# A two-layer block on one core: low-rank paths of the time mix from unmixed features, keys before the other products

## The chip, the cores and the metric

The kernel runs on one core of a Trainium2 chip. TensorE multiplies, VectorE (DVE), ScalarE (ACT) and GpSimd (POOL) do the elementwise work, and transfers from HBM are issued mostly on the queue of SyncE (SP). The metric is the device time of one execution in microseconds; before the change the median of three runs was 1236.0 us (1233.78 to 1236.62).

## The reference

256 tokens of 1024 features pass through two blocks in float32: the first has latent attention with retention, cross-attention to 256 memory rows and a mixture of 32 experts; the second has an attention and pooling mixer, a gated feed-forward layer, an RWKV-7 time mix, and a second feed-forward layer. The change lies in the time mix and at the join of the two blocks. Cut to what matters there:

```python
xx = _token_shift(h) - h
xr, xw, xk, xv, xa, xg = [h + xx * mu[i] for i in range(6)]
r, k, v = xr @ w_r, xk @ w_k, xv @ w_v                 # 1024 x 1024 each
w = -softplus(-(w0 + tanh(xw @ w1) @ w2)) - 0.5        # decays, rank 64
a = sigmoid(a0 + (xa @ a1) @ a2)                       # rates, rank 64
g = sigmoid(xg @ g1) @ g2                              # gate, rank 160
kk = k * k_k / max(norm(k * k_k), 1e-12)               # by heads of 64
k = k * (1 + (a - 1) * k_a)
decay = exp(-exp(w))
# per token and head: state = state * decay + (state @ -kk) (kk * a)^T + v k^T;  y = state @ r
y = group_norm(y) * ln_w + ln_b + sum(r * k * r_k) * v
return (y * g) @ w_o
```

## The kernel before

Features stand with the 1024 features over partitions in eight blocks of 128 and the 256 tokens along the free axis ("feature-major"). A fast product is made of three single-pass products (`mm3`): each operand is split into a rounded part, which ScalarE casts to fp32r (line 363), and a rest, which VectorE subtracts (line 364); where `self.sub` is set, POOL does. `mm` on operands left in float32 is one product, which leaves two records in the trace. Weights come through a ring of five raw buffers (`w`, `NRAW`) by `wchunk`, are split into `ws` buffers, and a product lands in one of four PSUM banks `acc` or four `ps`.

The time mix (from 773 us) norms x, transposes it to hF and takes dF, the difference with the token before. The mixes h + xx * mu for the rates, the gate and v are made on POOL (`mix_apart`, lines 1504 and 1505), those for r, the decays and k on VectorE. The order written is: r, low ranks of decays and rates, gate, decays `sg`, rates `av`, their running sums and exponentials (`em`, `ep`, `be`), then k chunk by chunk with the removal of its part along kk (`k_evac`), with v's chunks in between. Tokens are cut into chunks of 64, those into blocks of 32. L, the products of keys with keys inside the blocks, is turned by a stream transpose (`Ll`), and the unit triangular matrix I + L is inverted for all 128 blocks at once by a substitution of 31 steps with two VectorE operations each (`Xl`). The inverse is transposed back (`Lc`, then `X`), joined to the 64-wide inverse, and the chunk loop carries the state over four chunks. `ar` holds the decayed removal directions and r; `kb` the keys and the rates' keys; "products" (`p`) are kb with ar; "turned" (`t`) are transposes `BK`; "corners" (`c`) and the gate (`g`) are further generators.

Tile places instructions on each engine in the order that a simulated timeline gives; `behind` (`issue_after`) holds a piece back until a named instruction has been placed. Which step of which generator comes between the keys' chunks, the removals, the substitution's steps and the chunks is the table `BETWEEN`: a letter is one step. In the first block, the experts' last group (g == 7) is followed by a branch for tokens over an expert's 32 places (`overflow`, not taken with these inputs); SyncE takes part in it, and the next layer's weights `hy_w_in` were issued behind it.

Of the kernel before, what the change touches and what calls it, by code (L numbers as in the profile page):

```python
# [19 lines left out]
P = 128  # L20
# [189 lines left out]
class Block:  # L210
    def __init__(self, ctx, tc, I, C, out, dbg=None, phases="ABCDEFG"):
# [12 lines left out]
        self.held = {}  # L224
# [20 lines left out]
        if "C" in phases:  # L245
# [3 lines left out]
            with tc.tile_pool(name="pC", bufs=1, reuse_waits="tile") as self.pp:  # L249
                x = self.phase_c(x, o)  # L250
# [748 lines left out]
    def phase_c(self, x, o):  # L999
# [86 lines left out]
        for g in range(8):  # L1086
# [86 lines left out]
    def overflow(self, x, r, gain, over, acc):  # L1173
# [3 lines left out]

        raw = lambda n: self.wp.tile([P, CW], F32, tag="w", bufs=NRAW, name=self.nm("ow"))[:, :n]
# [281 lines left out]
    def phase_f(self, x, with_ffn):  # L1460
# [37 lines left out]
        def mix_apart(i):  # L1498

            f = Feat(self, 8, "k4", 8, side)  # L1500
            for b in range(0, 8, 2):
                xm = k4("xm", "uv", 2)[:, :512].rearrange("p (k c) -> p k c", k=2)
                m = mu[:, i * 8 + b : i * 8 + b + 2].unsqueeze(2).broadcast_to([P, 2, T])
# [3 lines left out]
            return f  # L1507

# [10 lines left out]
        def rows(ap, n, extra=None):  # L1519

            r = self.wp.tile([P, CW], F32, tag="w", bufs=NRAW, name=self.nm("w"))
            nc.sync.dma_start(r[:n], ap)
            m = n
            if extra is not None:
                nc.sync.dma_start(r[n : n + 1], extra.unsqueeze(0))
                m = n + 1
            return self.wsplit(r[:m].rearrange("p (k c) -> p k c", k=2))

        def small_split(n):
            return [self.pp.tile([P, T], F32R, tag=f"lo{s}", bufs=2, name=self.nm("lo"))[:n] for s in range(2)]  # L1530

        def low_rank(f, w1):
# [641 lines left out]
```

## Time and profile before

| | us |
|---|---|
| median of 3 runs | 1236.0 (1233.78 to 1236.62) |
| the profiled execution | 1233.26 |
| its span in the trace | 1231.5 |
| TensorE busy | 1127.2 (92%), 7070 records |
| VectorE, ScalarE, POOL busy | 703.1, 574.8, 219.8 |
| time mix, from the norm's first transpose to the chunk loop's first product | 773.9 to 964.9 |
| experts' output done, next layer's first product | 471.1, 475.3 |

The span is what the trace covers of the profiled execution; the 1.8 us around it belong to its time. TensorE records can overlap, so sums of their lengths are more than the time they take; an interval between starts is exact. The granted clock of a stretch is given as a share of full speed.

### The profile page before, as it was taken

Reading aid. Unit: us, or ns where it says so; the run is one execution under the profiler, and the core shown is the slowest. Engines: PE = TensorE matmul, PEld = TensorE weight load, DVE = VectorE, ACT = ScalarE, POOL = GpSimd, SP = SyncE. Lnnn points to the kernel's source line nnn. Section 1 sums busy time; section 2 is a strip of 40 time slices with the busy share of each in tenths; the row PEclk is TensorE's granted clock in tenths of the full one; section 3 lists DMA queues with packets and bytes.
Section 4 is the critical chain, followed back from the end, with each engine's and each line's share of the span. In section 5 each row is a group of like instructions: output and inputs, shape, how many; then the busy total and the mean of one; then the engine's idle time right before and its main releaser. Section 6 shows DMA issues by size and latency. Waiting matters only on the chain. (4 is left out here: it accounts for less than half of the span.)

```text
span 1231.5 us, 18724 instructions
## 1 busy us (share of the span) xinstructions
PE 1127.2 (92%) x7070; PEld 874.4 (71%) x7070; DVE 703.1 (57%) x1332; ACT 574.8 (47%) x1116; POOL 219.8 (18%) x192
## 2 busy tenths in 40 slices
PE   6999999979988878999999999678998989999998
PEld 5778878744333225888888888677976977888887
DVE  4978565541211105875766666895766556766665
ACT  5667555411000004684645454447675355555452
POOL 3101000000000010300100000587476820000000
PEclk9999999989999988999999999798996999999999
DMA  8533596889999995543556655033312114756661
GB/s 282 169 118 118 173 386 212 299 312 409 409 409 409 409 394 174 172 136 121 188 188 188 188 188 171 26 106 102 121 50 84 46 36 154 224 187 188 189 190 67
DMA packets 125153, 246.04 MB, mean 200 GB/s; under 512 B 11665, under 2 KB 66353, under 8 KB 125058
## 3 DMA queue, kind: packets, MB, share of 16 engines
q1 hardware_dynamic: 123250, 240.52, 56.6%
q0 software_dynamic: 1520, 4.01, 1.0%
q8 instruction: 57, 0.93, 0.3%
q10 hardware_dynamic: 288, 0.26, 0.1%
q14 instruction: 38, 0.31, 0.1%
HBM read 243.70 MB, written 1.05 MB: 199 GB/s over the span
## 5 line engine op out<-in xcount | busy, mean ns | idle before, releaser
L364 DVE TENSOR_TENSOR ws<-w,ws 128x1024 fp32r<-128x1024 f32 (+5 forms) x341 | 329.0, 979 | 161.1 <-ACT ws L363 160.2
L363 ACT CAST ws<-w 128x1024 fp32r<-128x1024 f32 (+6 forms) x365 | 288.2, 804 | 222.1 <-issue 83.8
L312 PE MATMUL ps<-fp,ws 128*128 128x512 f32 (+1 forms) x1472 | 255.1, 334 | 0.2
L312 PEld LDWEIGHTS ps<-fp,ws 128*128 128x128 f32 x1472 | 221.9, 190 | 31.3 <-DVE fp L187 0.6
L312 PE MATMUL acc<-ws,f 128*128 128x512 f32 (+1 forms) x696 | 177.5, 408 | 13.6 <-ACT ws L363 7.4
L312 PEld LDWEIGHTS acc<-ws,f 128*128 128x128 f32 x696 | 132.3, 195 | 44.2 <-ACT ws L363 9.0
L326 ACT ACTIVATE s<-ps 128x256 f32<-128x256 f32 (+2 forms) x114 | 47.0, 414 | 217.7 <-PE ps L312 217.7
L312 PE MATMUL acc<-ws,h 128*128 128x512 f32 x528 | 124.1, 391 | 0.0
L312 PEld LDWEIGHTS acc<-ws,h 128*128 128x128 f32 x528 | 97.7, 188 | 21.0
L312 PE MATMUL acc<-f,ws 128*128 128x256 f32 x480 | 70.9, 304 | 16.5 <-DVE ws L364 10.2
L312 PE MATMUL ps<-we,xs 128*32 128x512 f32 x512 | 77.1, 606 | 3.4 <-DMA we<-in_experts_dram 2.0
L312 PEld LDWEIGHTS acc<-f,ws 128*128 128x128 f32 x480 | 65.6, 207 | 19.7 <-DVE ws L364 12.1
L347 POOL TENSOR_TENSOR rs_r<-rs_v,mhalf 128x2 f32<-128x2 f32 (+3 forms) x26 | 24.4, 944 | 301.8 <-DVE kan L338 181.8
L1112 DVE TENSOR_TENSOR xs<-ps,cols 128x256 f32<-128x256 f32 x32 | 13.6, 425 | 101.6 <-PE ps L312 101.5
L312 PE MATMUL acc<-ws,o 128*128 128x512 f32 x192 | 48.1, 406 | 1.3 <-ACT ws L363 1.2
L312 PEld LDWEIGHTS ps<-Pm,x 128*128 128x128 f32 x256 | 32.2, 200 | 23.0 <-issue 18.8
L312 PE MATMUL acc<-ws,mf 128*128 128x512 f32 x192 | 47.9, 399 | 0.0
L329 DVE TENSOR_TENSOR s<-ps,s 128x256 f32<-128x256 f32 x80 | 33.5, 421 | 24.5 <-ACT s L326 24.5
L312 PE MATMUL ps<-we,hT 128*32 128x512 f32 x256 | 36.9, 622 | 10.5 <-DMA rowD<-in_rowD_dram 6.7
L312 PEld LDWEIGHTS ps<-we,xs 128*32 128x32 f32 x512 | 15.6, 110 | 42.0 <-issue 25.9
L312 PEld LDWEIGHTS acc<-ws,o 128*128 128x128 f32 x192 | 36.3, 193 | 10.1 <-ACT ws L363 1.6
L347 POOL TENSOR_TENSOR rx<-rs_v,mhalf 128x2 f32<-128x2 f32 x6 | 7.3, 1208 | 191.9 <-DVE rs_v L338 106.3
(406 smaller groups left out, 1481.6 us busy)
## 6 DMA issues: line engine op xcount, KB each, us to landing
we<-in_experts_dram SPq DMA_DIRECT2D x192, 512.0 KB, 10.2
w<-in_ffn_w_gate_dram SPq DMA_DIRECT2D x44, 512.0 KB, 4.3
w<-in_ffn_w_up_dram SPq DMA_DIRECT2D x44, 512.0 KB, 3.7
w<-in_ffn_w_down_dram SPq DMA_DIRECT2D x44, 512.0 KB, 3.6
w<-in_hy_w_in_dram SPq DMA_DIRECT2D x20, 512.0 KB, 3.8
w<-in_w_in_dram SPq DMA_DIRECT2D x16, 512.0 KB, 4.6
w<-in_cross_w_kv_dram SPq DMA_DIRECT2D x16, 512.0 KB, 3.6
w<-in_rw_w_o_dram SPq DMA_DIRECT2D x10, 512.0 KB, 3.6
```

Source lines behind the costliest of these rows:

```text
L312: return self.nc.tensor.matmul(out, lhsT, rhs, start=start, stop=stop, skip_group_check=True)
L326: self.nc.scalar.activation(out, in_, func, **kw)
L329: self.nc.vector.tensor_tensor(out, a, b, op)
L347: self.rooted = self.nc.gpsimd.tensor_tensor(r, v, self.mhalf[:, :n], ALU.pow).ins
L363: i = self.nc.scalar.copy(a, src)
L364: j = (sub or self.nc.vector).tensor_tensor(b, src, a.bitcast(F32), ALU.subtract)
L1112: return nc.vector.tensor_tensor(xs[:, 2 * b : 2 * b + 2, :], ps.rearrange("p (k c) -> p k c", k=2), gb, ALU.mult)
```

## The change

The decays, rates and the gate are no longer taken from mixed and split features. Since (h + xx * mu) @ w = h @ w + xx @ (mu * w), their low-rank products are raw float32 products of hF with the weights and of dF with weights scaled by mu on VectorE (`scaled`); decays and rates share one 128-column pass. w2, a2, g2 and v are raw float32 products too, so their weights and features are not split. k and r stay split. Keys come first; r, v, the gate's second product, the products with kb and the turned matrices are steps between the substitution's. POOL no longer mixes or splits there. In the first block, the first four chunks of `hy_w_in` are issued ahead of the branch, whose code uses one weight buffer in place of several.

```diff
 BETWEEN = dict(
-    keys=("v", "", "", "v", "", "", "", "v"),
-    removals=("v", "v", "", ""),
-    substitution="vcvvpgpggtgtppgttppt",
-    chunks=(("", "", "tt"), ("p", "p", ""), ("", "", ""), ("", "", "")),
+    keys=("", "", "", "", "", "", "", ""),
+    removals=("r", "", "", ""),
+    substitution={0: "r", 4: "r", 8: "rc", 12: "r", 16: "r", 20: "r", 24: "r", 28: "pvpvpvtptvpvvvpvttggggtt"},
+    chunks=(("", "", ""), ("p", "p", ""), ("", "", ""), ("", "", "")),
 )
...
     def wchunk(self, w, k0, nk, c0, ncol):
 
+        if (k0, nk, c0, ncol) in self.early:
+            return self.early.pop((k0, nk, c0, ncol))
...
             if g == 7:
 
+                if with_next:
+
+                    new = {(k0, 2, 0, 512): self.wchunk(I["hy_w_in_2"][0], k0, 2, 0, 512) for k0 in (0, 2, 4, 6)}
+                    self.early.update(new)
+                ow = self.wp.tile([P, CW], F32, tag="w", bufs=NRAW, name=self.nm("ow"))
                 most = nc.values_load(mxi[0:1, 0:1], min_val=0, max_val=T)
                 with self.tc.If(most > 32):
-                    self.overflow(x, r, gain, over, acc)
+                    self.overflow(x, r, gain, over, acc, ow)
...
-        def mix_apart(i):
...
-                nc.gpsimd.tensor_tensor(xm, dF[:, b : b + 2, :], m, ALU.mult)
-                nc.gpsimd.tensor_tensor(xm, xm, hF[:, b : b + 2, :], ALU.add)
-                self.split_to(*f.blk(b, 2), xm, nc.gpsimd)
...
+        def scaled(r, parts):
+
+            nk = r.shape[1]
+            m = self.s2(nk * r.shape[2]).rearrange("p (k c) -> p k c", k=nk)
+            return m, [
+                nc.vector.tensor_tensor(
+                    m[:, :, c0 : c0 + n], r[:, :, c0 : c0 + n], mu[:, i * 8 + k0 : i * 8 + k0 + nk].unsqueeze(2).broadcast_to([P, nk, n]), ALU.mult
+                )
+                for i, k0, c0, n in parts
+            ]
...
+        ws = [scaled(wl[:, k0 : k0 + 4], ((1, k0, 0, 64), (4, k0, 64, 64)))[0] for k0 in (0, 4)]
+        pw = self.psb(T)
+        for k in range(8):
+            self.mm(pw, wl[:, k, :], hF[:, k, :], k == 0, False)
+        for k in range(8):
+            self.mm(pw, ws[k // 4][:, k % 4, :], dF[:, k, :], False, k == 7)
...
+        self.act(uw[:64], pw[:64], AF.Tanh)
+        nc.vector.tensor_copy(ua[64:], pw[64:])
+        fk = mix(2)
...
-                self.mm3(po, [q[:, t * P : (t + 1) * P] for q in uw], ws[c], True, True)
+                self.mm(po, uw[:, t * P : (t + 1) * P], w2[:65, c * 512 : c * 512 + 512], True, True)
...
+        def r_evac(j, ps):
+            sl = slice(2 * j, 2 * j + 2)
+            bo = self.s2(512)
+            self.tt(arx(1, sl), p3(ps), fl(ep[:, sl, :, 1:65]), ALU.mult)
             nc.gpsimd.tensor_tensor(p4(bo), f4(ar[:, sl, :, 1, :]), keys(sl), ALU.mult)
...
+        fv = [self.pp.tile([P, D], F32R, tag=f"f{s}", bufs=self.nf, name=self.nm("fv")).bitcast(F32).rearrange("p (k c) -> p k c", k=4) for s in (0, 1)]
+        for k in range(8):
+            self.stt(fv[k // 4][:, k % 4, :], dF[:, k, :], mu[:, 24 + k : 25 + k], hF[:, k, :], ALU.mult, ALU.add)
...
+                        for f_, w_ in ((hF, r[:, k1 + k]), (dF, m[:, k])):
+                            self.mm(pg[:, t], f_[:, kk, t * P : (t + 1) * P], w_, kk == 0 and t == 0 and f_ is hF, kk == 7 and f_ is dF)
...
+        def values():
+            for c in range(2):
+                ps = [self.psa(512) for _ in range(2)]
+                for k0 in range(0, 8, 2):
+                    w = self.wchunk(I["w_v"], k0, 2, c * 512, 512)
+                    for k in (k0, k0 + 1):
+                        for t in range(2):
+                            self.mm(ps[t], fv[k // 4][:, k % 4, t * P : (t + 1) * P], w[:, k - k0], k == 0, k == 7)
...
-        steps = {"v": chain.from_iterable(aside(self.lin_tm_g(fv, I["w_v"], c * 512, 512, 8, v_evac(c))) for c in range(2))}
+        steps = {"v": values(), "r": self.lin_fm_g(fr, I["w_r"], 0, D, 8, r_evac)}
...
+        pr2 = self.psb(512)
+        for s in range(31):
...
+            self.tt(pr, Lp[s // 16][:, m:, s % 16 : s % 16 + 1].broadcast_to([P, n, m]), Xl[:, s : s + 1, 0:m].broadcast_to([P, n, m]), ALU.mult)
+            self.tt(Xl[:, m:, 0:m], Xl[:, m:, 0:m], pr, ALU.add)
+            with self.behind(last.ins, self.scaled):
+                run(BETWEEN["substitution"].get(s, ""))
```

On SyncE's queue at the join of the blocks, before (`we` are experts' weights, `rowD`, `band` and `pw` small tables of the next layer, the branch follows):

```order
L995 DMA we_3820<-in_experts_dram 128x1024
L995 DMA we_3832<-in_experts_dram 128x1024
L1353 DMA rowD_4171<-in_rowD_dram 128x128
L1436 DMA band_4172<-c_pool_dram 128x1536
L1437 DMA pw_4173<-in_hy_pool_w_dram 128x4x128
L1144 COMPARE_AND_BRANCH
```

and now:

```order
L998 DMA we_3820<-in_experts_dram 128x1024
L998 DMA we_3832<-in_experts_dram 128x1024
L388 DMA w_3968<-in_hy_w_in_dram 128x2x512
L388 DMA w_3970<-in_hy_w_in_dram 128x2x512
L388 DMA w_3972<-in_hy_w_in_dram 128x2x512
L388 DMA w_3974<-in_hy_w_in_dram 128x2x512
L1360 DMA rowD_4172<-in_rowD_dram 128x128
L1443 DMA band_4173<-c_pool_dram 128x1536
L1444 DMA pw_4174<-in_hy_pool_w_dram 128x4x128
L1152 COMPARE_AND_BRANCH
```

Four 512 KB transfers moved ahead of the three tables and the branch. On VectorE at the start of the substitution, before (`Ll` is the turned L, `ps` the step's product, `Xl` the inverse being built):

```order
L1709 COPY bon<-ps_8139 128x2x4
L1758 STREAM_TRANSPOSE Ll_8147<-Lc_8145 128x1024
L329 TENSOR_TENSOR ps_8290<-ps_8286,Xl_8148 128x31
L329 TENSOR_TENSOR Xl_8148<-Xl_8148,ps_8290 128x31
L329 TENSOR_TENSOR ps_8290<-ps_8286,Xl_8148 128x60
L329 TENSOR_TENSOR Xl_8148<-Xl_8148,ps_8290 128x30x2
L329 TENSOR_TENSOR ps_8290<-ps_8286,Xl_8148 128x87
L329 TENSOR_TENSOR Xl_8148<-Xl_8148,ps_8290 128x29x3
```

and now:

```order
L1758 STREAM_TRANSPOSE Ll_7567<-Lc_7565 128x1024
L365 TENSOR_TENSOR ws_7758<-w_7751,ws_7757 128x512
L330 TENSOR_TENSOR ar<-acc_7609,k_1664_7031 128x8x64
L330 TENSOR_TENSOR ps_7702<-ps_7691,Xl_7568 128x31
L330 TENSOR_TENSOR Xl_7568<-Xl_7568,ps_7702 128x31
L330 TENSOR_TENSOR ps_7702<-ps_7691,Xl_7568 128x60
L365 TENSOR_TENSOR ws_7796<-w_7793,ws_7795 128x512
L330 TENSOR_TENSOR Xl_7568<-Xl_7568,ps_7702 128x30x2
L365 TENSOR_TENSOR ws_7800<-w_7793,ws_7799 128x512
L330 TENSOR_TENSOR ps_7702<-ps_7691,Xl_7568 128x87
L330 TENSOR_TENSOR Xl_7568<-Xl_7568,ps_7702 128x29x3
L365 TENSOR_TENSOR ws_7918<-w_7915,ws_7917 128x512
```

Splits of r's weights (`ws`) stand between the steps, which before followed each other alone. On ScalarE around the copies of the solved blocks (`X`), before (`gt` and `BK` are the gate and the turned matrices, `k` with accumulators `acc` the products with kb):

```order
L326 ACTIVATE BK_8353<-acc_8584 128x512
L326 ACTIVATE gt_8544<-acc_8546 128x512
L326 ACTIVATE gt_8545<-acc_8568 128x512
L326 ACTIVATE BK_8353<-acc_8598 128x512
L326 ACTIVATE k_1962_8606<-acc_8608 64x4x64
L326 ACTIVATE k_1962_8606<-acc_8608 128x4x64
L326 ACTIVATE k_1962_8606<-acc_8609 64x4x64
L326 ACTIVATE k_1962_8606<-acc_8609 128x4x64
L326 ACTIVATE X_8689<-Lc_8145 32x16x32
L1874 COPY X_8689<-Lc_8145 32x16x32
L326 ACTIVATE X_8689<-Lc_8145 32x16x32
L1874 COPY X_8689<-Lc_8145 32x16x32
```

and now:

```order
L327 ACTIVATE k_1835_8108<-acc_8110 128x4x64
L327 ACTIVATE k_1835_8108<-acc_8111 64x4x64
L327 ACTIVATE k_1835_8108<-acc_8111 128x4x64
L327 ACTIVATE X_8327<-Lc_7565 32x16x32
L1870 COPY X_8327<-Lc_7565 32x16x32
L327 ACTIVATE X_8327<-Lc_7565 32x16x32
L1870 COPY X_8327<-Lc_7565 32x16x32
L327 ACTIVATE X_8328<-Lc_7565 32x16x32
L1870 COPY X_8328<-Lc_7565 32x16x32
L327 ACTIVATE X_8328<-Lc_7565 32x16x32
L1870 COPY X_8328<-Lc_7565 32x16x32
L327 ACTIVATE k_1835_8108<-acc_8132 64x4x64
```

The copies of `X` now stand ahead of the gate, of all turned matrices and of most of the products.

## Rows read from the trace of the kernel before

**Rows 1.** The page: busy time by engine, and the chain that ended last.
```profile
PE 1127.2 (92%) x7070; PEld 874.4 (71%) x7070; DVE 703.1 (57%) x1332; ACT 574.8 (47%) x1116; POOL 219.8 (18%) x192
...
PE 25%; DVE 5%; ACT 1%; POOL 1%; issue 1%; POOLq 0%; ACTq 0%; DVEq 0%
```

**Rows 2.** Four windows of the time mix: stretch, length, busy time, granted clock, DMA.
```profile
773.00:820.00 47.00, 31.29 (x192) 29.07 (x192) 42.74 (x50) 18.99 (x37) 34.35 (x27) 0.82 0.17 46
820.00:905.00 85.00, 76.97 (x533) 70.57 (x533) 59.99 (x81) 59.90 (x125) 58.98 (x45) 0.94 0.37 118
905.00:940.00 35.00, 30.38 (x373) 22.54 (x373) 24.20 (x65) 22.07 (x49) 27.98 (x24) 0.84 0.16 54
940.00:965.00 25.00, 23.95 (x369) 20.72 (x369) 8.59 (x10) 14.85 (x32) 16.81 (x11) 0.61 0.13 44
```

**Rows 3.** Waits, 773 to 965: engine, tile, releaser: us, times, longest.
```profile
PE acc L312 <- DVE ws L364: 10.2, 8, 2.3
...
PE ps L312 <- ACT ws L363: 4.2, 1, 4.2
PE acc L312 <- POOL ws L364: 4.1, 3, 2.8
```

**Rows 4.** Timeline, TensorE: start, us, operation, out<-in, count of records.
```profile
463.11 0.19 PEld L312 LDWEIGHTS acc<-s,pgT 128*128 128x128 f32 x1 [0.24 <-issue]
463.54 0.19 PEld L312 LDWEIGHTS acc<-s,pgT 128*128 128x128 f32 x1 [0.24 <-issue]
...
858.22 1.05 PE L312 MATMUL ps<-c_cum,sg 128*128 128x130 f32 x8
...
861.66 3.95 PE L312 MATMUL acc<-f,ws 128*128 128x256 f32 x31
...
1099.74 4.95 PE L312 MATMUL acc<-ws,h 128*128 128x512 f32 x21
```

**Rows 5.** Timeline, TensorE: norm, L products, first product of the chunk loop.
```profile
773.92 5.69 PE L312 MATMUL ps<-diag,x 128*128 128x128 f32 x32 [1.95 <-DVE ssn L329]
...
904.94 3.62 PE L312 MATMUL ps<-ar,kb 64*64 64x64 f32 x128
...
964.93 1.26 PE L312 MATMUL ps<-R,X 128*64 128x64 f32 x18
```

**Rows 6.** VectorE: groups (795:905, then 865:905), then the timeline of the substitution.
```profile
L364 DVE TENSOR_TENSOR ws<-w,ws 128x512 fp32r<-128x512 f32 x31 | 27.9, 920 | 11.6 <-ACT ws L363 11.6
L332 DVE SCALAR_TENSOR_TENSOR s<-k,cols,k 128x256 f32<-128x256 f32 x16 | 10.9, 732 | 0.0
L364 DVE TENSOR_TENSOR f<-s,f 128x512 fp32r<-128x512 f32 x9 | 10.8, 1221 | 0.1
...
L364 DVE TENSOR_TENSOR ws<-w,ws 128x512 fp32r<-128x512 f32 x11 | 7.3, 682 | 0.0
...
915.83 0.20 DVE L329 TENSOR_TENSOR ps<-ps,Xl 128x31 f32<-128x31 f32 x1 [0.66 <-ACT ps L1761]
...
939.16 0.19 DVE L329 TENSOR_TENSOR Xl<-Xl,ps 128x31 f32<-128x31 f32 x1
939.38 1.93 DVE L1845 STREAM_TRANSPOSE Lc<-Xl 128x1024 f32<-128x1024 f32 x1
```

**Rows 7.** ScalarE: a table load, the last exponentials; POOL: a group of masks.
```profile
842.00 1.28 ACT L326 ACT_TABLE_LOAD   x1
...
861.94 0.67 ACT L326 ACTIVATE k<-ps 128x260 f32<-128x260 f32 x2 [0.37 <-PE ps L312]
...
L1792 POOL TENSOR_TENSOR k<-k,c_gmask 64x1024 f32<-64x1024 f32 x3 | 7.1, 2352 | 0.1
```

**Rows 8.** Timeline around the join of the experts' layer and the next.
```profile
464.04 12.82 SPq L385 DMA_DIRECT2D w<-in_hy_w_in_dram  x6
...
470.37 0.69 DVE L329 TENSOR_TENSOR x<-acc,x 128x512 f32<-128x512 f32 x1 [0.17 <-PE acc L312]
...
475.26 2.05 PE L312 MATMUL acc<-ws,f 128*128 128x512 f32 x3 [3.27 <-ACT ws L363]
```

More of the change, by code (lines that the diff above doesn't have):

```diff
@@ L1550, in phase_f @@
-        fa = mix_apart(4)
-        fg = mix_apart(5)
-        ar = side.tile([P, 4096], F32, name="ar").rearrange("p (i c x t) -> p i c x t", i=8, c=4, x=2)
-        fr = mix(0)
-        fw = self.new_f()
-        pr = [self.psa(512) for _ in range(4)]
-        for k in range(8):
-            raw = self.wchunk(I["w_r"], k, 1, 0, D)
-            for j in range(4):
-                if j % 2 == 0:
-                    w = self.wsplit(raw[:, :, j * 256 : j * 256 + 512])[0]
-                self.fm_acc(pr[j], [[a[:, j % 2 * 256 : j % 2 * 256 + 256] for a in w]], fr, k, 1, 8)
-            if k in range(1, 5, 1):
-                with self.behind(*self.last_split):
-                    mix(1, fw, (2 * (k - 1) // 1,))
@@ L1701, in k_evac @@
             self.tt(keys(sl), p4(am), f4(em[:, sl, :, 1:65]), ALU.mult)
+        def r_evac(j, ps):
+            sl = slice(2 * j, 2 * j + 2)
+            bo = self.s2(512)
+            self.tt(arx(1, sl), p3(ps), fl(ep[:, sl, :, 1:65]), ALU.mult)
             nc.gpsimd.tensor_tensor(p4(bo), f4(ar[:, sl, :, 1, :]), keys(sl), ALU.mult)
             sums.append((j, bo))
-            if j:
+            for _ in range(0 if j == 0 else 1 if j < 3 else 2):
                 bonus()
@@ L1717, in aside @@
-        def aside(steps):
-            self.sub = nc.gpsimd
-            for _ in steps:
-                self.sub = None
+            self.tt(fl(be[:, sl]), fl(av[:, sl]), fl(em[:, sl, :, 1:65]), ALU.mult)
+        fr = mix(0, Feat(self, 8, "k4", 8, side))
+        fv = [self.pp.tile([P, D], F32R, tag=f"f{s}", bufs=self.nf, name=self.nm("fv")).bitcast(F32).rearrange("p (k c) -> p k c", k=4) for s in (0, 1)]
+        for k in range(8):
+            self.stt(fv[k // 4][:, k % 4, :], dF[:, k, :], mu[:, 24 + k : 25 + k], hF[:, k, :], ALU.mult, ALU.add)
@@ new lines, in phase_f @@
+        pg = self.psb(320).rearrange("p (t c) -> p t c", t=2)
+        for k0, nk in ((0, 6), (6, 2)):
+            r = self.wchunk(I["g1"], k0, nk, 0, 160)
+            for k1 in range(0, nk, 3):
+                n = min(3, nk - k1)
+                m, _ = scaled(r[:, k1 : k1 + n], ((5, k0 + k1, 0, 160),))
+                for k in range(n):
+                    kk = k0 + k1 + k
+                    for t in range(2):
+                        for f_, w_ in ((hF, r[:, k1 + k]), (dF, m[:, k])):
+                            self.mm(pg[:, t], f_[:, kk, t * P : (t + 1) * P], w_, kk == 0 and t == 0 and f_ is hF, kk == 7 and f_ is dF)
@@ L1840, in phase_f @@
         steps["t"] = chain.from_iterable(turned(c) for c in range(3))
-        steps["g"] = aside(gate())
-        with self.behind(last.ins, self.scaled):
-            run(BETWEEN["substitution"])
+        steps["g"] = gate()
+        pr2 = self.psb(512)
+        for s in range(31):
+            n, m = 31 - s, s + 1
+            at = s % 2 * 256
+            pr = pr2[:, at : at + n * m].rearrange("p (a b) -> p a b", a=n)
+            self.tt(pr, Lp[s // 16][:, m:, s % 16 : s % 16 + 1].broadcast_to([P, n, m]), Xl[:, s : s + 1, 0:m].broadcast_to([P, n, m]), ALU.mult)
+            self.tt(Xl[:, m:, 0:m], Xl[:, m:, 0:m], pr, ALU.add)
+            with self.behind(last.ins, self.scaled):
+                run(BETWEEN["substitution"].get(s, ""))
         YC = k8(0)[:, :D].rearrange("p (a b) -> p a b", a=32)
```

123 lines of the change are left out of this document (42 added, 81 removed).

## The prediction

> **What bounds the kernel now.** I read the page's head first: TensorE is busy 92% of the span, and the chain that ended last is mostly its own work; where anything else ends a wait there, it is a VectorE split or a ScalarE cast [rows 1]. The reader should see that the time can fall in two ways only: less idle time or a better clock on TensorE, since its work hardly can. Next came the stretches of the time mix, 773 to 965 us, from the first transpose of its norm to the first product of the chunk loop [rows 2, 5]. In 192 us TensorE is busy 162.6, so 29.4 us are idle. The granted clock is 0.82, 0.94, 0.84 and 0.61 in the four stretches [rows 2]; busy time times the missing share is 31.29 x 0.18 + 76.97 x 0.06 + 30.38 x 0.16 + 23.95 x 0.39 = 24 us that full clock would not have taken. So the stretch holds about 138 us of work at full clock and 54 us of losses. Third, the waits of that stretch: TensorE's go to VectorE's splits (10.2 us), to a cast (4.2) and to POOL's splits (4.1) [rows 3]. Last, the join of the experts' layer with the next: SyncE issues its first pool-mixer weight at 464.04, the layer's output is done at 470.37 + 0.69 = 471.1, and the first product on those weights starts at 475.26 after 3.27 us behind a cast [rows 8].
>
> **The change, part by part.**
>
> *More TensorE work.* In fp32r a 256-column product takes 3.95 / 31 = 0.127 us and a 512-column one 4.95 / 21 = 0.236 [rows 4]. A raw float32 product leaves two records; those of 512 columns start 463.54 - 463.11 = 0.43 apart, so 0.86 a product, and 256 columns 0.43 [rows 4]. The small form agrees: 8 records of 130 columns in 1.05, 0.13 each [rows 4]. Removed, by the code's counts: 96 + 12 + 24 split products of 512 columns (v, w2, g2), 132 x 0.236 = 31.2; and 24 + 24 + 48 + 24 of up to 256 (w1, a1, g1, a2), 120 x 0.127 = 15.2; together 46.4. Added: v 32 x 0.86 = 27.5, g2 8 x 0.86 = 6.9, w2 4 x 0.86 = 3.4, w1 with a1 16 x 0.43 = 6.9, a2 8 x 0.43 = 3.4, gate 32 of 160 columns at 2 x 0.13 x 160/130 = 0.32, hence 10.2 at most and 8.6 by the 512-column price (I take 9), its transposes 0.6; together 57.7. Net +11.3, and 1.2 for two more turned matrices that fall into this stretch: +12.5. If nothing else moved the kernel would be 12.5 us slower; all that follows is about the 54 us of losses.
>
> *The decays come early (gain).* Before, the decays' exponentials end at 861.94 + 0.67 = 862.6 [rows 7], and the k path, which needs them, lets the L products start at 904.94 and end at 908.5 [rows 5]. Afterwards r stands behind k. Transposes of h end near 781.8: before they end at 773.92 + 5.69 = 779.6 [rows 5], the last copy follows by 1, and four scaled multiplies stand ahead of one small step on VectorE (1.2). The 16 low-rank products take 6.9: 789. The rates' low-rank copy stands on VectorE behind k's mix, eight multiply-adds (0.732 at the pace of before) and four splits (1.221) [rows 6], 10.7 us, most of it started before 789: 795. Then w2 and a2 with their sigmoids to about 805, exponentials (16 halves at 0.33 plus a table load of 1.28 [rows 7] and waits) to 813, the gate's products, with some of k's between them, to 821. From there VectorE sets the pace: 16 splits of k's weights at 0.68 [rows 6], four evacuations of k with six operations of that size and two small ones each, 4.4, and 3 of waiting, 32 us: 853.5. L products 3.6 [rows 5], with what hides in between: about 858, against 908.5. TensorE's own share of k then (153 of 192 products left, 19.4, with 3 of r and 4 of head sums and transposes) fits inside.
>
> *From L's end to the chunk loop (loss).* Before, this leg took 964.93 - 908.5 = 56.4 us. Now TensorE has in it 168 products of r (21.3), v (27.5), the corners, head sums and k with k (6.6), the products with kb at full clock (10.2; before, about half of them ran in the stretch of clock 0.61 [rows 2]), the turned (3.6), g2 (6.9) and the merges (6.1): 82 us, with about 11 of waits and of clock, 93: 951. Beside it runs the substitution. Before, its 62 steps took from 915.83 to 939.35 without a break [rows 6]; now ten splits (6.8 at 0.68 [rows 6]), r's multiplies (2.8) and four small copies (0.6) stand between them on VectorE, a chain of about 34 us. It begins near 863, ends near 897 to 901, and two transposes of 1.93 [rows 6] are done by 905, while TensorE still has v and the products to do. So the chain, which before had only 20 us of TensorE work beside it at poor clock, is covered. Gain of the time mix: 964.9 - 951 = 14 us. In losses: 150.5 us of work in 178 us, so 28 in place of 54. I choose half because the start keeps its own waits (about 12 of low-rank chain and norm) and VectorE's pace in the k stage stays.
>
> *POOL's mixes and splits go.* They cost TensorE 4.1 us of waiting [rows 3], and VectorE more: the same split takes 0.682 in the stretch 865 to 905 and 0.920 on average from 795 on [rows 6]. The sum above already uses the short time. The Trainium skill, "SBUF — State Buffer", section "Who interferes with whom", says that a VectorE instruction with two inputs in SBUF contends with a GpSimd instruction that reads SBUF, and that one of the two then blocks entirely. The two means of rows 6 agree. By that rule the splits now put into the substitution have two such inputs, while POOL's group masks (2.35 each [rows 7]) fall near them; if each of the ten waited for half a mask it would be 12 us on the chain, which is the first rival's aggravation.
>
> *A fourth table load on ScalarE.* The gate's sigmoid stands apart from the other: 1.28 us [rows 7], beside TensorE work of the k stage: 0, or 1.3 if that cover is missing. The Trainium skill, "ScalarE: Activation LUTs", lists about 2.7 us for such a load; the trace's 1.28 decides, and with 2.7 the upper end would be 1.4 more.
>
> *Pool-mixer weights issued before the branch.* Their four transfers are in SBUF by 464; casts of them no longer wait at 475.26, so products may start when the features are there, about 472: up to -3.8. ScalarE's cast stands between feature copies, which then come later; half returns. On the other side rowD, band and pw are issued four transfers later (about 1.3 us each by SyncE's issue, 5 us), and SyncE's branch with them; if that made the fifth weight late I expect +2. I take -2.0, bounds -4 and +2. Nothing later than 475 was late in that stage.
>
> *Sum.* -14 - 2 = -16 on the profiled 1233.3, whose span is 1231.5; it lies 2.7 below the median, 1236.0, to which I apply it. By rows 7 I give back one for the table load: -15, hence 1221.
>
> **The rivals.** *The substitution becomes the bound (slower).* For: it is one chain in VectorE's order, with splits that wait for ScalarE's casts, which wait for TensorE to free the split buffers, and ScalarE's copies of the solved blocks now stand ahead of the remaining evacuations, so that four accumulator banks fill up and TensorE stops. If r runs at TensorE's pace between the steps, the chain takes 23.5 + 10.2 + 28 = 62 and ends at 926, with 4 of transposes and 5 more of copies 935, and 38 of TensorE's work is left: 973, 8 later than now, with -2 at the branch 1242. It decides from a chain end after about 916. Against: VectorE and TensorE do r at once, and 8 casts fit in 34 us. *The start stays bound by latency:* the low-rank chain leaves TensorE idle and at a low clock as now (0.82 over the first 47 us [rows 2]) and the decays come at 825 in place of 813; the 12 us come off the gain: -3 to -5, 1232. For it: every step of that chain crosses engines; against: VectorE has little else to do then. *The early issue costs:* +2 at the branch in place of -2, otherwise as forecast: 1225. *TensorE stays full:* losses of 15 in place of 28 because r and v are there whenever a step waits: -28, 1208.
>
> **How the numbers follow.** Forecast (with the branch either way, 1214 to 1229) 0.50; start stays bound, 1229 to 1235, 0.16; full, 1203 to 1214, 0.18; substitution bound, 1236 to 1250, 0.16. What a measurement of this kernel tells from no change is about 0.2%, 2.5 us. Slower by more: three quarters of the last case, 0.13; within: its rest and a quarter of the second, 0.07; faster 0.80. The range is 1204 to 1239, which leaves about 0.1 on the slow side and less on the fast; the likeliest case's own is 1214 to 1229.
>
> **What would show it.** Right: exponentials ended by about 815; L products ended near 858; the substitution about 34 us long and over well before TensorE reaches the first R product; clock above 0.9 where it was 0.61; POOL's busy time down by some 80 us; first pool-mixer product before 474. Wrong: a TensorE wait of several us for an evacuation or for Xl at the end of the substitution, TensorE rows of k or r waiting on splits for over 15 us in sum, or exponentials after 825.

## The result and the profile after

The changed kernel takes 1213.7 us in the median (1210.24 to 1214.91), a ratio of 0.982 with an interval of 0.980 to 0.984: 21 us faster than the kernel before, whose median, with one run more, is now 1234.9. Its profiled execution took 1214.54 with a span of 1212.8, which is 18.7 us less than before. On the page TensorE is busy for nearly the same time as before (1127.5 us for 1127.2), and POOL for 130.2 us in place of 219.8:

```profile
PE 1127.5 (93%) x7022; PEld 858.2 (71%) x7022; DVE 663.0 (55%) x1328; ACT 547.6 (45%) x1061; POOL 130.2 (11%) x132
```

The time mix in three windows (columns as in [rows 2]; before the substitution, beside it, behind it):

```profile
769.60:852.00 82.40, 76.24 (x582) 68.04 (x583) 49.84 (x102) 48.31 (x101) 9.21 (x14) 0.84 0.31 99
852.00:894.00 42.00, 37.15 (x355) 32.34 (x355) 33.94 (x82) 16.44 (x36) 6.00 (x5) 0.87 0.24 77
894.00:946.00 52.00, 52.00 (x477) 29.48 (x476) 9.21 (x11) 23.71 (x50) 29.76 (x23) 1.00 0.27 89
```

From the norm's first transpose to the first product of the chunk loop it now lasts 945.75 - 769.63 = 176.1 us in place of 964.93 - 773.92 = 191.0 [rows 5]. TensorE is idle 11.0 us of it, and the missing clock costs 76.24 x 0.16 + 37.15 x 0.13 = 17.0: losses of 28 in place of 54. Behind the substitution the engine is never idle and the clock is 1.00, where [rows 2] had 0.61. TensorE's longest waits for operands, against those of [rows 3]:

```profile
PE ps L313 <- DVE rs_v L339: 2.8, 1, 2.8
PE acc L313 <- DVE ws L365: 2.7, 3, 1.4
PE ps L313 <- DVE kb L330: 2.7, 1, 2.7
```

The timeline of TensorE that answers to [rows 5]:

```profile
769.63 5.50 PE L313 MATMUL ps<-diag,x 128*128 128x128 f32 x32 [2.82 <-DVE rs_v L339]
...
784.02 6.55 PE L313 MATMUL ps<-w,lo 65*128 65x512 f32 x8 [0.82 <-ACT lo L327]
790.50 7.19 PE L313 MATMUL ps<-lo,w 64*128 64x256 f32 x16
...
850.54 1.13 PE L313 MATMUL ps<-ar,kb 64*64 64x64 f32 x32 [2.66 <-DVE kb L330]
...
887.95 10.11 PE L313 MATMUL acc<-w,fv 128*128 128x512 f32 x20
...
945.75 0.92 PE L313 MATMUL ps<-R,X 128*64 128x64 f32 x13
```

The reader should see three things. w2 and a2 (784.02, 790.50) run near half clock: the granted clock of 784.0 to 797.7 is 0.53, and 8 records of 512 columns take 6.48, 0.81 each, nearly twice the 0.43 of [rows 4]. The L products end at 850.54 + 1.13 = 851.7, 82.0 behind the norm's first transpose; before it was 134.6. And v's first 20 records (887.95) last 10.1, 0.50 each. The last exponentials, on ScalarE, end at 807.2; [rows 7] had 862.6:

```profile
804.81 2.37 ACT L327 ACTIVATE k<-ps 128x260 f32<-128x260 f32 x8
```

The substitution on VectorE, first and last of its 62 steps, lasts 33.6 us in place of 23.5 [rows 6]:

```profile
860.58 0.19 DVE L330 TENSOR_TENSOR ps<-ps,Xl 128x31 f32<-128x31 f32 x1
...
893.97 0.19 DVE L330 TENSOR_TENSOR Xl<-Xl,ps 128x31 f32<-128x31 f32 x1
```

At the join (rows of SyncE's queue, TensorE and VectorE; compare [rows 8]):

```profile
450.43 4.21 SPq L388 DMA_DIRECT2D w<-in_hy_w_in_dram  x4
...
462.68 3.78 PE L313 MATMUL acc<-s,pgT 128*128 128x512 f32 x4 [0.71 <-ACT s L327]
...
469.15 7.67 SPq L388 DMA_DIRECT2D w<-in_hy_w_in_dram  x3
...
472.68 0.69 DVE L330 TENSOR_TENSOR x<-acc,x 128x512 f32<-128x512 f32 x1 [0.17 <-PE acc L313]
...
474.06 0.71 PE L313 MATMUL acc<-ws,f 128*128 128x512 f32 x2
```

Four weights are issued at 450.43, ahead of the branch; those behind it come at 469.15, 5 us later than before. The experts' output is done at 473.4, 2.3 us later than before. The first product then starts 0.69 us behind it, where it took 4.20 before, and so 1.2 us earlier in the span. Behind it TensorE is busy 28.35 of 30 us at a clock of 1.00; before (second row), the same window had 26.27 and 0.89:

```profile
470.00:500.00 30.00, 28.35 (x138) 22.77 (x139) 23.59 (x39) 22.62 (x37) 10.33 (x13) 1.00 0.56 162
...
470.00:500.00 30.00, 26.27 (x117) 21.05 (x117) 20.40 (x35) 19.80 (x32) 5.84 (x8) 0.89 0.51 156
```

At full clock that is 28.35 us of work for 26.27 x 0.89 = 23.4, so 5 us more were done there.

The 2.3 us by which the output came later are not the change's. The four products that combine the experts take 3.78 us in this trace (462.68), and took 1.98 in the trace before:

```profile
462.58 1.98 PE L312 MATMUL acc<-s,pgT 128*128 128x512 f32 x4 [0.71 <-ACT s L326]
```

In both, TensorE has just stood idle for 6.7 us at the branch; over the 8 us behind that its granted clock is 0.50 here and 0.83 before. Both values occur with and without the early issue: of the runs below, the kernel without it has 0.50 and the one with the gate's product early has 0.82. So the output is the better point to count from. From there to the norm's first transpose it takes 296.3 us in place of 302.9, 6.6 less.

Counted from the start of the span, 4.3 of the 18.7 us were there when the time mix began (769.63 against 773.92), 14.9 came in it, and 0.5 went behind it.

### The profile page after: what moved, and what is told of

Read it like the earlier page. It is cut to its first block, busy times and chain, and to the rows that moved or that the text cites. A ratio compares the mean times of both kernels' runs of the same rounds, so it can differ in the third digit from the quotient of the medians.

```text
span 1212.8 us, 18457 instructions
## 1 busy us (share of the span) xinstructions
PE 1127.5 (93%) x7022; PEld 858.2 (71%) x7022; DVE 663.0 (55%) x1328; ACT 547.6 (45%) x1061; POOL 130.2 (11%) x132
## 4 chain that ended last, share of the span: by engine, by line
PE 71%; DMA 12%; issue 9%; DVE 4%; ACT 2%; POOL 1%; SPq 0%; POOLq 0%; DVEq 0%; ACTq 0%
PE acc L313 35%; PE ps L313 33%; DMA we<-in_experts_dram 10%; PE ps L324 2%; DVE ws L365 2%; DMA w<-in_w_in_dram 1%; ACT ws L364 1%; DMA w<-in_hy_w_in_dram 1%; DVE s L330 1%; ACT s L327 0%; ACT Lc L327 0%; POOL rs_r L348 0%; POOL diag L518 0%; POOL s L1669 0%; DMA w<-in_rw_w_k_dram 0%
## 5 line engine op out<-in xcount | busy, mean ns | idle before, releaser
L365 DVE TENSOR_TENSOR ws<-w,ws 128x1024 fp32r<-128x1024 f32 (+3 forms) x331 | 314.4, 962 | 162.4 <-ACT ws L364 154.3
L364 ACT CAST ws<-w 128x1024 fp32r<-128x1024 f32 (+3 forms) x335 | 270.7, 823 | 215.6 <-issue 83.7
L313 PE MATMUL acc<-ws,f 128*128 128x512 f32 (+1 forms) x696 | 173.6, 401 | 11.1 <-DVE ws L365 5.3
L313 PEld LDWEIGHTS acc<-ws,o 128*128 128x128 f32 x192 | 36.5, 194 | 10.1 <-ACT ws L364 1.6
L313 PE MATMUL acc<-f,ws 128*128 128x256 f32 x288 | 41.4, 295 | 0.7 <-ACT ws L364 0.7
L313 PEld LDWEIGHTS acc<-ws,mf 128*128 128x128 f32 x192 | 35.2, 188 | 6.9
L313 PE MATMUL acc<-s,pgT 128*128 128x512 f32 x64 | 32.4, 639 | 6.7 <-ACT s L327 6.7
L313 PEld LDWEIGHTS acc<-f,ws 128*128 128x128 f32 x288 | 37.3, 195 | 1.9 <-ACT ws L364 1.1
```

Of the source, the lines that this page charges most:

```text
L313: return self.nc.tensor.matmul(out, lhsT, rhs, start=start, stop=stop, skip_group_check=True)
L364: i = self.nc.scalar.copy(a, src)
L365: j = (sub or self.nc.vector).tensor_tensor(b, src, a.bitcast(F32), ALU.subtract)
```

## The experiments

All medians are put beside the kernel before, timed in the same set. The changed kernel, timed again with the last set, came to 0.9808 (0.9783 to 0.9834).

**The early issue alone, on the kernel before.**

```diff
...
+                if with_next:
+                    new = {(k0, 2, 0, 512): self.wchunk(I["hy_w_in_2"][0], k0, 2, 0, 512) for k0 in (0, 2, 4, 6)}
+                    self.early.update(new)
...
```

> The kernel before with one part of the change: the first four pool-mixer weights issued ahead of the branch, and one buffer in the branch's code. In the changed kernel the first product on these weights starts 1.2 us earlier and the granted clock of 470 to 500 us is 1.00 in place of 0.89, worth about 3 us more. Theory (both come from the early issue): 3 to 4.5 us faster than before, first product near 474 and clock 1.00 behind it. Rival (the clock is chance): 0 to 1.5 faster. Second rival (the three small tables and the branch come 5 us later and cost it again): 1 to 2 slower.

Ratio 0.9999 (0.9985 to 1.0013): no gain. The trace shows where it went (TensorE; POOL, as a timeline and as a group; VectorE twice; ScalarE; TensorE twice):

```profile
769.52 2.73 PE L312 MATMUL ps<-diag,x 128*128 128x128 f32 x20 [1.94 <-DVE ssn L329]
...
825.86 9.98 POOL L364 TENSOR_TENSOR k<-xm,k 128x512 fp32r<-128x512 f32 x2
...
L364 POOL TENSOR_TENSOR k<-xm,k x2: 1257/5008/8758, 825.9 to 834.6; 128x512 fp32r<-128x512 f32 x2
...
826.10 3.24 DVE L332 SCALAR_TENSOR_TENSOR s<-k,cols,k 128x256 f32<-128x256 f32 x8
...
832.21 1.28 DVE L364 TENSOR_TENSOR f<-s,f 128x512 fp32r<-128x512 f32 x2
...
839.08 0.62 ACT L363 CAST k<-xm 128x512 fp32r<-128x512 f32 x1 [8.41 <-POOL xm L1512]
...
840.27 2.08 PE L312 MATMUL ps<-ws,lo 65*128 65x512 f32 x4 [7.05 <-ACT ws L363]
...
965.05 1.15 PE L312 MATMUL ps<-R,X 128*64 128x64 f32 x16
```

The time mix begins at 769.52, as early as in the changed kernel, and its first chunk product comes at 965.05, as late as before. In between POOL begins two subtracts at 825.86 which take 9.98 us; the first takes 8.76, the second 1.26 (the row with least, median and largest duration in ns). From 826.10 to 833.5 VectorE runs sixteen operations with two inputs in SBUF, without a gap, and POOL's subtract ends 1.1 us behind the last of them. ScalarE's cast waits 8.41 for POOL, TensorE 7.05 for ScalarE. The last five products of w2 start at 842.74, only 1.2 us earlier than in the kernel before (843.98), so some 3 of the 4.4 us are given back there. The rest goes in the products around them: from 840.3 to 850.6, behind that wait, the clock is 0.50, where the kernel before had 0.83 (841.5 to 849.8). This is one trace of each kernel, and POOL's and ScalarE's order in this stretch is not quite the same in the two; that the whole gain is gone rests on the medians. None of the three theories had that: the first was right on the join (first product at 474.82, a clock of 1.00 behind it) and wrong on the time.

**The changed kernel without the early issue.**

```diff
-                if with_next:
+                if False:
```

> The changed kernel without that part. Theory: 3 to 4.5 us slower than the changed kernel, that is 16 to 18 faster than before, all of it in the time mix. Rival (clock by chance): at most 1.5 slower than the changed kernel.

Ratio 0.9876 (0.9859 to 0.9892): 15 us faster than before, 7 to 8 us by the ratios short of the changed kernel, 4.7 in the profiled spans. (The branch's code keeps its single buffer.)

```profile
477.70 2.91 PE L313 MATMUL acc<-ws,f 128*128 128x512 f32 x5 [3.27 <-ACT ws L364]
...
774.23 2.01 PE L313 MATMUL ps<-diag,x 128*128 128x128 f32 x9 [2.82 <-DVE rs_v L339]
...
949.25 0.92 PE L313 MATMUL ps<-R,X 128*64 128x64 f32 x13
```

First product at 477.70, norm at 774.23, chunk loop at 949.25: 175.0 us of time mix, as with the early issue. So the time mix alone gives 15 us, and the early issue is worth 5 to 8 in the changed kernel, more than the first theory's 3 to 4.5, and nothing in the old one. The traces agree on what it does at the join: in all twelve with the early issue the first product starts 0.69 us behind the experts' output and the norm 295.4 to 297.6 behind it; in the two without, 4.20, and 300.7 (this kernel) and 302.9 (the kernel before).

**r between the keys.**

```diff
-    keys=("", "", "", "", "", "", "", ""),
-    removals=("r", "", "", ""),
-    substitution={0: "r", 4: "r", 8: "rc", 12: "r", 16: "r", 20: "r", 24: "r", 28: "pvpvpvtptvpvvvpvttggggtt"},
+    keys=('', 'r', 'r', 'r', 'r', 'r', 'r', 'rr'),
+    removals=('', '', '', ''),
+    substitution={8: 'c', 28: 'pvpvpvtptvpvvvpvttggggtt'},
```

> The changed kernel with r's chunks between the keys' chunks, so that the substitution's 62 steps run without a break again. Theory (TensorE's work and its losses set the time of the time mix; the substitution is covered either way by v and the products): L products end some 25 us later, near 877, the substitution takes 24 us in place of 34, and the first product of the chunk loop comes within 3 us of the changed kernel's 945.75: the same time within 3 us. Rival (r beside the substitution is where the gain comes from): TensorE idles or runs at a low clock beside the bare substitution as it did before, 8 to 10 us slower than the changed kernel.

Ratio 0.9798 (0.9779 to 0.9816), within the changed kernel's interval.

```profile
770.03 2.27 PE L313 MATMUL ps<-diag,x 128*128 128x128 f32 x15 [2.82 <-DVE rs_v L339]
...
869.15 0.69 PE L313 MATMUL ps<-ar,kb 64*64 64x64 f32 x32 [1.01 <-DVE kb L330]
...
937.73 0.92 PE L313 MATMUL ps<-R,X 128*64 128x64 f32 x13
...
937.70:984.00 46.30, 43.68 (x665) 41.70 (x664) 19.72 (x68) 17.43 (x38) 19.78 (x17) 0.89 0.16 53
```

The L products end at 869.8, 99.8 behind the norm; the substitution takes 23.5 us (878.57 to 902.08), and the chunk loop begins 167.7 behind the norm in place of 176.1. That is 8 us earlier and more than the theory's 3; but from there to the first product of the output projection TensorE takes 46.3 us, idle for 2.6 and at a clock of 0.89, where the changed kernel takes 40.9 at 1.00. r's place does not matter to the time by more than the intervals tell; the rival, 8 to 10 us slower, is refuted.

**Decays and rates split as before.** Mixes on POOL (rates) and VectorE (decays), three products each; all else as changed.

```diff
-        for k in range(8):
-            self.mm(pw, wl[:, k, :], hF[:, k, :], k == 0, False)
...
+        fa = mix_apart(4)
+        fw = mix(1)
+        uw = low_split(low_rank(fw, I["w1"]), AF.Tanh, 65)
+        ua = low_split(low_rank(fa, I["a1"]), AF.Copy, 64)
```

> The changed kernel with the decays' and rates' products as before: mixed features (rates' on POOL, decays' on VectorE), split in three products each; the order of everything behind is the changed one. Theory (unmixed features bring the decays early, and that is worth more than the products cost): the exponentials end 10 to 14 us later, L products end 8 to 12 later, 7 to 10 us slower than the changed kernel. Rival (the latency is hidden and only TensorE's work counts): 2 to 3 us faster than the changed kernel, because the split products are cheaper.

Ratio 0.9932 (0.9913 to 0.9952): some 14 us slower than the changed kernel; its profiled run is the fastest of six, and its span only 8.7 longer.

```profile
767.45 1.72 PE L313 MATMUL ps<-diag,x 128*128 128x128 f32 x11 [1.95 <-DVE ssn L330]
...
816.61 0.77 ACT L327 ACTIVATE k<-ps 128x260 f32<-128x260 f32 x2
...
859.21 1.34 PE L313 MATMUL ps<-ar,kb 64*64 64x64 f32 x40 [2.87 <-DVE kb L330]
...
954.36 0.92 PE L313 MATMUL ps<-R,X 128*64 128x64 f32 x13
```

Counted from the norm's first transpose the exponentials end 49.9 behind it in place of 37.6, L products 93.1 in place of 82.0, the chunk loop begins 186.9 in place of 176.1. The 11 us of delay pass through to the chunk loop undiminished. The theory's mechanism and its delays hold; its total, 7 to 10, fits the spans and is too small for the medians. That split products are cheaper for TensorE does not show. POOL is not held up here: its mixes and subtracts take 1.3 to 1.6 us each on average, which leaves the longer path to the low ranks, through mixes, casts and splits, for the delay.

**The gate's first product early.**

```diff
...
+        pg = self.psb(320).rearrange("p (t c) -> p t c", t=2)
...
         fk = mix(2)
...
-        pg = self.psb(320).rearrange("p (t c) -> p t c", t=2)
...
```

> The changed kernel with the gate's low-rank products, sigmoid and transposes moved ahead of k's mix, so that TensorE does them while the decays' and rates' chain waits; in the changed kernel they run from 807.6 to 816.2, and w2 and a2 run at half clock from 784 to 797.6. Theory (TensorE's idle time and half clock at the start are what is left to take): about 8 us faster than the changed kernel, w2 and a2 at 0.43 a record of 512 columns in place of 0.82, L products ended near 843. Rival (VectorE's splits and evacuations of k set the pace after the decays): 2 to 3 faster only, the time comes back as waits for splits of k.

Ratio 0.9866 (0.9842 to 0.9890): no gain, but some 6 us slower than the changed kernel, and the intervals do not touch. The profiled run is the fastest of five, and its span, 1212.4, is that of the changed kernel, so the trace shows why nothing is gained and not where the 6 us go.

```profile
769.30 5.41 PE L313 MATMUL ps<-diag,x 128*128 128x128 f32 x32 [4.22 <-DVE rs_v L339]
...
792.67 3.15 PE L313 MATMUL ps<-w,lo 65*128 65x512 f32 x4
...
850.36 0.81 PE L313 MATMUL ps<-ar,kb 64*64 64x64 f32 x40 [2.35 <-DVE kb L330]
```

w2 starts at 792.67, 8.65 later than in the changed kernel, and w2 and a2 still run near half clock: 8 records and 16 of half the width from 792.67 to 806.51, beside one of k, at 0.52, although TensorE was busy for 21.4 of the 23.3 us before, at 0.93. So filling its idle time ahead of them did not bring them to full clock. The gate's work was put in front of the chain on which all waits, not beside it: L products end 81.9 behind the norm, as in the changed kernel. Neither theory holds: TensorE's waits for splits of k come to 2 us from 784 to 860, too little to have taken the gain back.

**v as split products.**

```diff
+        fv = mix(3)
...
-                            self.mm(ps[t], fv[k // 4][:, k % 4, t * P : (t + 1) * P], w[:, k - k0], k == 0, k == 7)
...
+        steps = {"v": chain.from_iterable(self.lin_tm_g(fv, I["w_v"], c * 512, 512, 8, v_evac(c)) for c in range(2)), ...
```

> The changed kernel with v as split products (features and weights split on ScalarE and VectorE) at the same place in the order. Theory (behind the substitution TensorE works at full clock with VectorE idle, so its work sets the time): 96 products at 0.236 in place of 32 at 0.86, 4 to 5 us faster than the changed kernel. Rival (VectorE has no room beside the keys and the substitution, and two more splits stand in its chain): 0 to 4 slower.

Ratio 0.9850 (0.9824 to 0.9875): 4 to 5 us slower than the changed kernel by the ratios, whose intervals overlap at the edge. ScalarE's casts now wait for TensorE to free the split buffers (from 852 to 945; in the changed kernel 7.1 us):

```profile
ACT ws L364 <- PE acc L313: 18.5, 13, 2.5
```

From L's end to the chunk loop it takes 92.6 us in place of 94.1; 1.5 of the expected 4 to 5 are gained, and 2.7 are lost behind it. The rival is nearer.

**Both of these edits.**

```diff
...
+        pg = self.psb(320).rearrange("p (t c) -> p t c", t=2)
...
         fk = mix(2)
...
+        fv = mix(3)
...
```

> Both edits of the two kernels before. Theory: the sum of the two, about 12 us faster than the changed kernel. Rival: no more than the better of the two.

Ratio 0.9896 (0.9873 to 0.9920), 9 to 11 us slower than the changed kernel. The theory is wrong, and the rival holds only by its words: it is worse than either edit alone. In its profiled span of 1222.6 the time mix takes 176.8 us up to the chunk loop (774.22 to 950.99), as in the changed kernel; 4.6 us are lost ahead of it, where none of the edits is, and 4.6 behind. Of those ahead, 3.3 were there when the first pool-mixer weights were issued (453.74 against 450.43), and the changed kernel's own second trace has 2.7 of them (453.12), so they are no sign of the edits. Why it loses behind stays open.

**Sixteen more POOL multiplies.**

```diff
             run(s)
+            for _ in range(2):
+                nc.gpsimd.tensor_tensor(UV[2][:, :512].rearrange("p (k c) -> p k c", k=2), hF[:, 0:2], hF[:, 2:4], ALU.mult)
```

> The changed kernel with 16 more POOL multiplies of 128 x 512 with two inputs in SBUF, two behind each chunk of the keys; what they write is overwritten before it is read. In the kernel with only the early issue a POOL subtract of 1.26 us took 8.76 while VectorE ran two-input operations without a gap. Theory (an operation of one of the two engines holds the other up when both read two inputs): VectorE's splits of k rise from 0.68 to 0.9 or more on average, POOL's multiplies above 1.3, and the kernel is 2 to 5 us slower than the changed one. Rival (only POOL is held up): VectorE's splits stay at 0.68 and the time is the same within 1 us.

Ratio 0.9975 (0.9960 to 0.9989): all but 3 us of the gain are gone. The scheduler put them not beside the keys but where hF is first complete, at the start of the time mix, beside VectorE's mixes (TensorE, VectorE, POOL, TensorE, TensorE):

```profile
772.53 1.72 PE L313 MATMUL ps<-diag,x 128*128 128x128 f32 x11 [2.60 <-DVE ssn L330]
...
790.96 8.53 DVE L333 SCALAR_TENSOR_TENSOR s<-k,cols,k 128x256 f32<-128x256 f32 x6
...
792.25 9.77 POOL L1736 TENSOR_TENSOR UV<-k 128x512 f32<-128x512 f32 x7
...
867.76 1.34 PE L313 MATMUL ps<-ar,kb 64*64 64x64 f32 x40 [2.27 <-DVE kb L330]
...
962.62 0.92 PE L313 MATMUL ps<-R,X 128*64 128x64 f32 x13
```

Six multiply-adds take 8.53 us, 1.42 each; in the changed kernel they take 2.46. POOL's own multiplies beside them take 1.40 each, against 1.26 to 1.29 for those of r later on, at the same pace as the multiply-adds, so here the two engines seem to have taken turns. A VectorE operation on 128 x 2 takes 1.22 (at 786.76) in place of 0.16. L products end 96.6 behind the norm in place of 82.0 and the chunk loop begins at 190.1, almost the 191.0 of the kernel before. Splits of k, far behind, stay at 0.69. Both engines are held up, as the theory said, VectorE far more than POOL, at another place and at about four times its highest price.

**Sixteen POOL memsets in their place.**

```diff
-                nc.gpsimd.tensor_tensor(UV[2][:, :512].rearrange("p (k c) -> p k c", k=2), hF[:, 0:2], hF[:, 2:4], ALU.mult)
+                nc.gpsimd.memset(UV[2], 1.0)
```

> As the kernel with 16 more POOL multiplies, but 16 POOL memsets of 128 x 1024 in their place, which read nothing; what they write is overwritten before it is read. They stand at the same place of POOL's order. Theory (two engines that both read two SBUF inputs hold each other up; POOL's mere activity does not): VectorE's multiply-adds of 128 x 256 stay near 0.41 where they took 1.42 beside the multiplies, L products end some 82 us after the norm's first transpose in place of 96.6, and the time is within 2 us of the changed kernel. Rival (POOL being busy, or the order that the scheduler makes of it, is what costs): 10 us or more slower, as with the multiplies.

Ratio 0.9803 (0.9779 to 0.9827): nothing lost. POOL is as busy at the same place, the six multiply-adds beside it take 2.46, and L products end 78.7 behind the norm (POOL, VectorE, VectorE):

```profile
775.02 12.08 POOL L1736 MEMSET UV<- 128x1024 f32 x12
...
777.05 0.99 DVE L337 TENSOR_SCALAR k<-k 128x2 f32<-128x2 f32 x1
...
783.40 2.46 DVE L333 SCALAR_TENSOR_TENSOR s<-k,cols,k 128x256 f32<-128x256 f32 x6
```

So it is POOL's reading that holds VectorE up, not that POOL is busy or in what order it stands. Only the tiny operation on 128 x 2 still takes up to 0.99.

**Products earlier, with r between the keys.**

```diff
-    substitution={8: 'c', 28: 'pvpvpvtptvpvvvpvttggggtt'},
+    substitution={0: 'pp', 4: 'pp', 8: 'c', 28: 'pvpvtvtvvvvvttggggtt'},
```

> The kernel with r between the keys, with four of the products' steps at the substitution's first steps and the other two before v. In the kernel with r between the keys the first product of the chunk loop came 167.7 us after the norm's first transpose in place of 176.1, and the end of the trace 272.5 behind it in place of 267.1, because POOL's masks and copies were late in the chunk loop. Theory: products and masks come 8 to 10 us earlier, the chunk loop does not stall, 4 to 6 us faster than with r between the keys (about 1206). Rival (the tail after the first product is set by v and by POOL's masks wherever they start): the same time within 2.

Ratio 0.9828 (0.9804 to 0.9853), slower than with r between the keys if anything. The chunk loop begins at 946.48, 175.4 behind the norm (771.12).

**All six products between the steps.**

```diff
-    substitution={0: 'pp', 4: 'pp', 8: 'c', 28: 'pvpvtvtvvvvvttggggtt'},
+    substitution={4: 'pp', 8: 'cpppp', 28: 'vvtvvtvvvvttggggtt'},
```

> The same with all six products' steps between the substitution's steps 4 and 8 and v in one piece behind. Theory: as the kernel before, 4 to 6 us faster than with r between the keys; TensorE's idle time beside the start of the substitution goes. Rival (v, which must wait for four accumulators to be freed, comes late and ends last): 2 to 4 slower than the kernel with four products first.

Ratio 0.9810 (0.9784 to 0.9835). Here it is 174.8 (767.97 to 942.77).

Both theories on the tail are wrong, and so is the second rival: the chunk loop started later and then did not stall (in the first of them TensorE is busy all of 946.4 to 990.0, at 1.00). From the norm to the first product of the output projection it takes 216.6 and 218.1 us in these two, 214.0 with r between the keys and 217.0 in the changed kernel; the first rival, the same time, is nearest. None of the variants is faster than the changed kernel by more than the intervals tell.

**The changed kernel again.**

> The changed kernel itself, timed beside the others of this set, as what they are compared with: 0.982 of the kernel before, between 0.980 and 0.984.

Ratio 0.9808 (0.9783 to 0.9834), as expected. Its trace tells how far a single trace can be trusted:

```profile
772.32 3.87 PE L313 MATMUL ps<-diag,x 128*128 128x128 f32 x32 [2.82 <-DVE rs_v L339]
...
945.33 0.92 PE L313 MATMUL ps<-R,X 128*64 128x64 f32 x13
```

The norm begins 2.7 us later than in the first trace of the same kernel, and so do the first weights' issue and the experts' output. The time mix takes 173.0 in place of 176.1: its transposes take 3.87 us and not 5.50, w2's eight records 5.21 and not 6.55; the clock of the first 14.7 us is 1.00, where the first 14.4 us had 0.88. The spans, 1212.4 and 1212.8, agree although the parts differ by 3 us. Differences of that size between two traces, in the time mix too, show nothing by themselves.

## Why the prediction was right, and where not

- **The time mix, -14.** It measured -14.9 in the profiles, -18.0 in the second trace of the changed kernel, and -15 in the medians without the early issue. The working held: exponentials at 813 against 807.2, L products at 858 against 851.7 (from a norm that began 4.3 earlier; 82.0 behind it against 84.1), 93 us from there to the chunk loop against 94.1, losses of 28 against 28. Of work at full clock there were 10 us more (165.4 busy less 17.0, against 162.6 less 24.4) where 12.5 were forecast, and they were outweighed. Undoing the low ranks alone takes back 11 of it; how the other 4 divide among the gate, v, the keys' place and POOL, no run tells.
- **The substitution, 34 us.** It took 33.6, but partly by luck. Three of its ten splits, those beside POOL's multiplies of r, took 1.43, 1.76 and 1.68 us where 0.68 was counted for each, 2.8 in all; as much was saved elsewhere: one of r's four multiplies came before the first step, and records that stand between two steps overlap them a little (by 0.07 at 861.22), where the bare steps had gaps of 0.04.
- **The join, -2 with bounds of -4 and +2.** This is the term that was mis-sized. The later branch (5 us) stands in the trace and cost nothing that shows. The step "half returns" was wrong: behind the experts' output all 3.5 us of the wait are gained (4.20 to 0.69), and nothing comes back. So was "Nothing later than 475 was late in that stage": in the 30 us behind it TensorE had idled and run at 0.89, and with the early issue it runs at 1.00. Counted from the experts' output the early issue gives 4.5 us (against the kernel without it) to 7.5 (alone, on the kernel before), and by the spans and the ratios 5 to 8 in the changed kernel. Why the clock is 1.00 there I cannot show beyond that TensorE is busier.
- **The table load, +1.** The fourth load is there (at 807.98, 1.28 us), but ScalarE waits 7.25 us for TensorE behind it, so it cost nothing.
- **POOL's work.** I priced it by TensorE's waits (4.1) and by VectorE's slower splits. The traces show a price that I left out, POOL itself held up behind VectorE, on a chain that TensorE waits for: before, two of its operations beside VectorE's mix take 6.50 us and ScalarE waits 3.59 for them; in the early-issue kernel one takes 8.76.

```profile
827.57 6.50 POOL L1505 TENSOR_TENSOR xm<-xm,k 128x512 f32<-128x512 f32 x2
...
834.11 0.62 ACT L363 CAST k<-xm 128x512 fp32r<-128x512 f32 x1 [3.59 <-POOL xm L1505]
```

What part of the 14.9 us this was is not shown; the run with the low ranks split as before lost 11 with ScalarE waiting 0.5 us for POOL in all. In the other direction sixteen POOL multiplies put almost all of the time mix's gain back. The Trainium skill, "SBUF — State Buffer", section "Who interferes with whom", says that only the pair of ports that the two engines share causes contention, and that it is an exclusive lock; a VectorE instruction with two SBUF inputs contends with a GpSimd instruction that reads SBUF, not with one that only writes it. The runs agree: 1.42 beside multiplies, 0.41 beside memsets, and a blocked POOL subtract of 8.76. I used that page only for the rival, the splits in the substitution; there POOL's masks came after the chain (from 902.3), and only its multiplies of r met the splits.
- **The forecast and the rivals.** The sum gave 1221, and 1213.7 was measured, inside the range. It lies 0.3 below the likeliest case's own bounds, among the times given to "TensorE stays full", and that is not what happened: the losses are the 28 us forecast, not 15. Most of the 7 us are the join's; the table load has one, and another is the median before, now 1.1 lower than the one the sum was taken from. The substitution as the bound did not happen: it ended at 894, and TensorE did not wait for it. r's place between its steps, which I told as part of the gain, is worth nothing by itself. The start bound by latency is partly true: w2 and a2 still run near half clock, but the decays came at 807, not 825. The early issue costing 2 did not happen. Of the signs, one was missed by a hair: the first pool-mixer product came at 474.06, not before 474, because the experts' output was late in that trace.

What stays open: why the gate's product early, and v split beside it, lose 6 to 11 us; and why the clock behind the branch is 0.50 in some traces and 0.83 in others of the same code.

## What to carry to other kernels

Before pricing work that leaves an engine which is "off the chain", look at the longest single durations of its instructions: one that takes several times its usual time is blocked by something, and the work behind it may be on the chain. A gain ahead of such a chain can be given back in it, so an edit that is worth nothing alone can be worth several us beside another. Where one engine's work sets the time, moving that work about on it gained nothing here; shortening what it waited for did. And before two traces are compared, count from the last event that the change cannot have touched, and look whether the clock ahead of it was the same: here it hid 2.3 us of a gain of 6.6.

## What the runs showed of the hardware

A POOL subtract of 128 x 512, 1.26 us when nothing stops it, took 8.76 while VectorE ran sixteen two-input operations back to back, and ended 1.1 us after the last: it was not let in between two of them. Beside a run of POOL multiplies it went otherwise: VectorE's multiply-adds went from 0.41 to 1.42 and POOL's multiplies to 1.40, one pace for both, as if they took turns. Beside POOL memsets the multiply-adds stayed at 0.41. What decides between the two cases the runs do not show. Behind the same idle stretch of some 6.7 us at the branch, in the same code, TensorE's granted clock over the next 8 us was 0.50 in ten traces and 0.81 to 0.83 in four, worth 2.3 us. A float32 product of 512 columns took 0.86 at full clock (v's later records agree: 24 from 912.43 to 922.93, 0.44 each, two a product) against 0.71 for the three fp32r products that replace it (3 x 0.236). So splitting saves TensorE some 17% there; for v that was less than its casts and subtracts cost in this stretch.
